# GpSimd's subtraction of weight parts in 128-column instructions, in a two-layer attention and retention trunk

## The chip, the cores and the metric

The kernel runs on one core of a Trainium2 chip. The metric is the device time of one execution in microseconds (us); the median of several runs is compared.

## The reference

Two layers of a decoder trunk over 528 rows (16 learned meta rows ahead of 512 real ones) of width 1024, all in float32. Cut to what matters:

```
h = concatenate([meta, x])                       # (528, 1024)
for each of 2 layers:
    proj = rmsnorm(h) @ w_in                     # 1024 -> 3592 columns
    fq, fk, fv, flog, rq, rk, rv, rg = split(proj)
    fox = softmax(fq fk^T / 8 + c[t] - c[s], causal) fv     # 8 heads of 64; c = cumsum(log_sigmoid(flog + b))
    ret = groupnorm((rotate(rq) rotate(rk)^T * decay) rv)   # 4 heads of 128
    h = h + concatenate([fox, silu(rg) * ret]) @ w_out
    hn = rmsnorm(h)
    h = h + (silu(hn @ w_gate) * (hn @ w_up)) @ w_down      # 1024 -> 2816 -> 1024
return rmsnorm(h)[16:]
```

## The kernel before, in words

Activations lie transposed in SBUF: eight tiles `h0` to `h7` of 128 features by 528 rows. A product is made exact enough by splitting each operand into a high part, rounded to TensorE's fast float32 form, and a low part, the rest. Three products are summed in PSUM: high weights by high activations (`whi`, `xh`), high by low (`whi`, `xl`) and low by high (`wlo`, `xh`).

Weights come in jobs. A job is a block of 128 output columns: 8 slices of 128 by 128, 1024 columns in SBUF. `dense_steps` makes a job and the steps of its 8 slices (`chunk`), `convert` fetches and splits it. For a job:

- SP issues the load of 512 KB into one of three `raw` buffers (`fetch`, L153). It waits until the buffer's former job is split.
- ScalarE rounds the first four slices (128x512) into `whi`, and later the other four (L186).
- The low part is `raw` less `whi`, again for four slices at a time (L187). GpSimd makes it for the jobs with `pool` set, which are nearly all projections of the attention half (`w_in`, part of `w_out`), 63 jobs in all. VectorE makes it for the others. `whi` and `wlo` have two buffers each.
- TensorE takes a slice at a time: `whi` by `xh`, `whi` by `xl`, `wlo` by `xh`, each in one or two parts of the rows (L210).

The split of a job is asked for while TensorE works on the job before it, at its second and its fifth slice (`ahead=(1, 4)`), so TensorE's first use lies some microseconds behind.

The order of TensorE's instructions is a list written out by hand, in which the steps of attention (`fox_steps`) and retention (`ret_steps`) are merged at chosen places among the slices of the projections. The other engines' orders come from a scheduler by priorities. Every engine runs its instructions in order and waits for the others by semaphores.

Names that the text speaks of: `R` is the rows' scale from the norm (L290, L293 on VectorE compute it, and the per-head `r` in the same way); `z` is the forget gate's logarithm, summed over the rows by L393 and written to DRAM as `cdr` (L395), from where it comes back spread over all partitions as `bc` (L487). `scores` adds `bc` to the scores and takes the row minimum `nmax` (L504, L509 joins two halves), and ScalarE takes the exponential (L517). `kl` is the low part of the attention keys (L443), `pd` holds values (L449), `vv` their transposes (L474), `ptl` the low part of the transposed probabilities (L138 in `split`). L613 is the rotation's last sum, L751 and L753 weigh the retention's output by its gate, L760 scales it, L778 adds to `h`.

The feed-forward halves split their weights on ScalarE and VectorE (L863, L864) and have no GpSimd work.

Of the kernel before, what the change touches and what calls it, by code (L numbers as in the profile page):

```python
# [10 lines left out]
F32 = mybir.dt.float32  # L11
# [28 lines left out]
def hybrid_kernel(ctx, tc, x_t, w_in, w_fl, w_out, w_gate, w_up, w_down, vecs, b_fg, rope, decay, mask, ident, out_t):  # L40
# [104 lines left out]
    def fetch(j):  # L145
        job = jobs[j]
        if "load" in job:
            job["load"]()
        elif "raw" not in job:
            n = job["src"].shape[1]  # L150
            job["raw"] = wp.tile([128, NK, 128], F32, name="raw", tag="raw", bufs=3)
            if j > 1:
                nc.sync.dma_start(job["raw"], job["src"]) if n == NK else \  # L153
                    nc.sync.dma_start(job["raw"][:, 0:n], job["src"])

    def wring(tag):
        pool = phase["ffn"] if tag[0] == "f" else wp
        return pool.tile([128, NK, 128], F32R, name=tag, tag=tag, bufs=2)

    def convert(j, upto=NK, pinned=False):  # L160

        if j >= len(jobs):
            return
        job = jobs[j]
        fetch(j)
        if "make" in job:
            if "w" not in job:
                n = job["n"]
                hi, lo = (wring(job["ring"] + p) for p in ("whi", "wlo"))
                job["w"] = [(NK, hi, lo)]  # L170
                job["make"](hi[:, 0:n], lo[:, 0:n])
            return
        n = job["src"].shape[1]
        if "w" not in job:
            job["w"] = job["own"]() if job["own"] else \
                [(NK, *[wp.tile([128, NK, 128], F32R, name=i, tag=i) for i in ("whi", "wlo")])]
            job["split"] = 0
        sub = nc.gpsimd.tensor_sub if job["pool"] else nc.vector.tensor_sub
        while job["split"] < min(n, upto):
            c0 = job["split"]  # L180
            c1 = min(n, c0 + (2 if j < 2 and c0 < 4 else 4))
            size, hi, lo = job["w"][c0 // job["w"][0][0]]
            o = c0 % size
            hi, lo = hi[:, o:o + c1 - c0], lo[:, o:o + c1 - c0]
            with tc.high_priority() if j == 5 else ExitStack():
                pin(nc.scalar.copy(hi, job["raw"][:, c0:c1]), pinned)  # L186
            pin(sub(lo, job["raw"][:, c0:c1], hi.bitcast(F32)), pinned)  # L187
            job["split"] = c1

    def dense_steps(src, parts, pool=False, banks=False, ahead=(1, 4), own=None, wait=None):  # L190
# [6 lines left out]
        def chunk(k0, k, n, xs, cols, ps, done):  # L197
            def go():
                convert(j)
                if k == 0:  # L200
                    t = [psum_a() for _ in cols] if banks else psum()
                    ps.append(t)
                    ps.append(t if banks else [t[:, b] for b in range(2)])
                size = jobs[j]["w"][0][0]
                _, hi, lo = jobs[j]["w"][(k0 + k) // size]
                wk = (k0 + k) % size
                xh, xl = xs(k)
                for i, (w, x) in enumerate(((hi, xh), (hi, xl), (lo, xh))):
                    for b, (c0, c1) in enumerate(cols):
                        nc.tensor.matmul(ps[1][b][:, 0:c1 - c0], w[:, wk, :], x[:, c0:c1],  # L210
                                         start=(k == 0 and i == 0), stop=(k == n - 1 and i == 2))
                if k == n - 1:
                    done(ps[0]) if wait is None else wait.append(lambda: done(ps[0]))
                for half, at_step in enumerate(ahead):
                    if k0 + k == at_step:
                        convert(j + 1, 4 * half + 4)
            return go
# [82 lines left out]
    def pin(f, pinned=True):  # L300
        if pinned:
            tc.keep_in_program_order(f)
# [485 lines left out]
    def ffn(l, st, real, last):  # L788
# [68 lines left out]
        def need(j):  # L857
            for i in range(j, min(j + 3, len(jobs))):
                if i <= j or "make" in jobs[i]:
                    convert(i)  # L860
# [542 lines left out]
```

## Time and profile before

| what | value |
|---|---|
| time, median of 3 runs | 1278.69 us (1278.58 to 1278.84) |
| the profiled execution: time | 1278.89 us |
| the profiled execution: span of the records | 1277.1 us |
| TensorE busy | 1258.0 us |
| VectorE busy | 1019.4 us |
| ScalarE busy | 687.7 us |
| GpSimd busy | 181.0 us, 172.3 of it in the 126 subtracts of L187 |
| mean granted TensorE clock | 0.996 |

In a row of instructions stand the line, the engine, the operation, what it writes and reads, and its size. Behind it come the total, the mean in ns, and the idle time just before, with what ended it. In a row of the timeline stand the start, the duration and the count, and in brackets the idle time before and what ended it. PE is TensorE, PEld its weight loads, DVE VectorE, ACT ScalarE, POOL GpSimd, SPq the queue of SP, which issues the DMAs. Rows of one instruction that follow each other are merged in the timeline (x2), the start being the first one's.

### The profile page before, as it was taken

What the parts mean: (1) busy time and instruction counts of PE and PEld (TensorE: products, weight loads), DVE (VectorE), ACT (ScalarE), POOL (GpSimd) and SP (SyncE); (2) the same over time, 40 slices, a digit from 0 to 9 for tenths busy, and PEclk for the clock granted to TensorE, in tenths of its full rate; (3) what the DMA queues carried; (4) which work ended last, traced back from release to release, by engine and by line L of the source; (5) the groups of instructions that cost most, each with busy time, mean ns of one, the idle gap of its engine ahead of it and who ended that gap; (6) DMA issues with size and microseconds to landing.
All of it is one profiled execution on the core that took longest, in us unless ns stands there. A gap on an engine that the chain in (4) does not pass through costs nothing.

```text
span 1277.1 us, 23190 instructions
## 1 busy us (share of the span) xinstructions
PE 1258.0 (99%) x9265; PEld 1197.8 (94%) x9265; DVE 1019.4 (80%) x1849; ACT 687.7 (54%) x1250; POOL 181.0 (14%) x150
## 2 busy tenths in 40 slices
PE   9999999999999999999999999999999999999997
PEld 8899999999999999999999989999789999999996
DVE  7888866879988888887687878568899878888867
ACT  7566655576544444444455665456764444444445
POOL 2233333210000000000014334332000000000001
PEclk9999999999999999999999999999999999999998
DMA  6222222223323333332323122222223333333321
GB/s 233 76 67 84 75 84 84 66 73 115 107 97 100 100 100 100 100 100 83 100 76 112 65 100 84 77 91 66 100 83 130 102 100 100 100 100 100 103 79 67
DMA packets 45677, 120.55 MB, mean 94 GB/s; under 512 B 5360, under 2 KB 12272, under 8 KB 45568
## 3 DMA queue, kind: packets, MB, share of 16 engines
q1 hardware_dynamic: 45136, 118.77, 28.4%
q8 instruction: 73, 1.20, 0.4%
q10 hardware_dynamic: 432, 0.29, 0.1%
q14 instruction: 36, 0.29, 0.1%
HBM read 116.91 MB, written 2.13 MB: 93 GB/s over the span
## 4 chain that ended last, share of the span: by engine, by line
PE 84%; DVE 10%; ACT 4%; DMA 1%; issue 1%; DVEq 0%; POOL 0%; ACTq 0%
PE psd L210 24%; PE psa L875 18%; PE psd L1010 14%; PE psd L875 13%; PE psa L1010 4%; PE psa L210 3%; PE psa L409 2%; PE psa L497 1%; PE psa L567 1%; PE psa L724 1%; PE psa L694 1%; DVE qs L429 1%; DMA bc<-cdr 1%; DVE pr L504 1%; DVE rsl L138 0%
## 5 line engine op out<-in xcount | busy, mean ns | idle before, releaser
L187 POOL TENSOR_TENSOR wlo<-raw,whi 128x512 fp32r<-128x512 f32 x126 | 172.3, 1381 | 380.2 <-ACT whi L186 380.2
L210 PE MATMUL psd<-xh,whi 128*128 128x264 f32 (+1 forms) x792 | 195.8, 315 | 0.0
L210 PE MATMUL psd<-xl,whi 128*128 128x264 f32 (+1 forms) x792 | 186.5, 303 | 0.6 <-DVE xl L313 0.6
L210 PE MATMUL psd<-xh,wlo 128*128 128x264 f32 (+1 forms) x792 | 186.9, 303 | 0.0
L210 PEld LDWEIGHTS psd<-xh,whi 128*128 128x128 f32 x792 | 128.7, 190 | 4.7 <-ACT whi L186 0.4
L210 PEld LDWEIGHTS psd<-xh,wlo 128*128 128x128 f32 x792 | 127.2, 188 | 6.2 <-DVE wlo L187 0.4
L210 PEld LDWEIGHTS psd<-xl,whi 128*128 128x128 f32 x792 | 128.0, 189 | 5.2 <-DVE xl L313 1.2
L186 ACT CAST whi<-raw 128x512 fp32r<-128x512 f32 (+1 forms) x168 | 98.3, 613 | 39.2 <-PE psd L210 19.9
L863 ACT CAST whi<-raw 128x1024 fp32r<-128x1024 f32 (+2 forms) x62 | 54.9, 885 | 51.3 <-PE psd L875 39.9
L863 ACT CAST fwhi<-raw 128x1024 fp32r<-128x1024 f32 (+2 forms) x62 | 55.6, 897 | 48.1 <-PE psd L875 40.5
L864 DVE TENSOR_TENSOR wlo<-raw,whi 128x1024 fp32r<-128x1024 f32 (+2 forms) x62 | 62.9, 1014 | 13.7 <-ACT whi L863 13.6
L864 DVE TENSOR_TENSOR fwlo<-raw,fwhi 128x1024 fp32r<-128x1024 f32 (+2 forms) x62 | 64.0, 1032 | 10.8 <-ACT fwhi L863 10.5
L875 PE MATMUL psa<-th,whi 128*128 128x264 f32 (+1 forms) x232 | 65.4, 282 | 0.0
L875 PE MATMUL psa<-th,wlo 128*128 128x264 f32 (+1 forms) x232 | 65.4, 282 | 0.0
L875 PE MATMUL psa<-tl,whi 128*128 128x264 f32 (+1 forms) x232 | 65.3, 282 | 0.0
L875 PE MATMUL psa<-th,fwhi 128*128 128x264 f32 (+1 forms) x224 | 63.4, 283 | 0.0
L875 PE MATMUL psa<-tl,fwhi 128*128 128x264 f32 (+1 forms) x224 | 63.3, 283 | 0.0
L875 PE MATMUL psa<-th,fwlo 128*128 128x264 f32 (+1 forms) x224 | 63.3, 282 | 0.0
L517 ACT ACTIVATE pr<-pr,nmax 128x144 f32<-128x144 f32 (+1 forms) x64 | 36.9, 576 | 42.8 <-DVE nmax L504 30.5
L941 ACT COPY e<-psa 128x264 f32<-128x264 f32 (+1 forms) x114 | 42.9, 376 | 27.9 <-PE psa L875 23.6
L863 ACT CAST fwhi<-S 128x1024 fp32r<-128x1024 f32 x20 | 21.0, 1049 | 68.6 <-PE psa L875 66.5
L1010 PE MATMUL psd<-ah,fwlo 128*128 128x264 f32 (+1 forms) x200 | 56.6, 330 | 0.0
(355 smaller groups left out, 4008.6 us busy)
## 6 DMA issues: line engine op xcount, KB each, us to landing
raw<-w_in SPq DMA_DIRECT2D x54, 512.0 KB, 3.5
raw<-w_gate SPq DMA_DIRECT2D x44, 512.0 KB, 4.0
fraw<-w_up SPq DMA_DIRECT2D x38, 512.0 KB, 3.4
raw<-w_down SPq DMA_DIRECT2D x64, 256.0 KB, 2.7
raw<-w_out SPq DMA_DIRECT2D x16, 512.0 KB, 3.5
raw<-w_down SPq DMA_DIRECT2D x32, 192.0 KB, 2.5
bc<-cdr SPq DMA_DIRECT2D x16, 264.0 KB, 3.3
raw<-w_up SPq DMA_DIRECT2D x6, 512.0 KB, 3.5
```

Source lines behind the costliest of these rows:

```text
L186: pin(nc.scalar.copy(hi, job["raw"][:, c0:c1]), pinned)
L187: pin(sub(lo, job["raw"][:, c0:c1], hi.bitcast(F32)), pinned)
L210: nc.tensor.matmul(ps[1][b][:, 0:c1 - c0], w[:, wk, :], x[:, c0:c1], start=(k == 0 and i == 0), stop=(k == n - 1 and i == 2))
L409: nc.tensor.transpose(ps[:, 128 * j:128 * j + 128], src[:, o:o + 128], idt)
L429: nc.vector.tensor_sub(sv(t, real, b0, b1), sv(tq, real, a0, a1), sv(t, real, a0, a1).bitcast(F32))
L497: nc.tensor.matmul(sc[0:nq, 0:c1 - c0], st["q"][s][:, q0:q0 + nq], kk[:, c0:c1], start=(i == 0), stop=(i == 1))
L517: nc.scalar.activation(pr, pr, AF.Exp, bias=nmax[0:nq], scale=-1.0, accum_out=rsum)
L863: nc.scalar.copy(hi, src)
L864: nc.vector.tensor_sub(lo, src, hi.bitcast(F32))
L875: nc.tensor.matmul(bank()[:, 0:b.shape[-1]], a[:, o + k, :], b, start=(fresh and k == 0 and i == 0), stop=(k == n - 1 and i == 2), skip_gr ...
L941: nc.scalar.copy(self.t["e"][:, i], self.t["x"][:, 0:w])
L1010: nc.tensor.matmul(v[:, 0:c1 - c0], a[:, s * n + k, :], b[:, c0:c1], start=(k == 0 and i == 0), stop=(k == n - 1 and i == 2))
```

## The change

Where GpSimd subtracts, the four slices of a half job are taken one by one: four instructions of 128x128 in the place of one of 128x512. VectorE's subtracts stay as they are.

```
-            pin(sub(lo, job["raw"][:, c0:c1], hi.bitcast(F32)), pinned)
+            step = 1 if job["pool"] else c1 - c0
+            for c in range(0, c1 - c0, step):
+                pin(sub(lo[:, c:c + step], job["raw"][:, c0 + c:c0 + c + step], hi[:, c:c + step].bitcast(F32)), pinned)
```

On GpSimd, the first job's two halves before (lines of the changed kernel are two higher from here on):

```order
L187 TENSOR_TENSOR wlo<-raw,whi 128x512 [waits DVE_49,DMAHW1_49,PE_49,Activation_49]
L187 TENSOR_TENSOR wlo<-raw,whi 128x512 [waits Activation_49]
L187 TENSOR_TENSOR wlo<-raw,whi 128x512 [waits DVE_49,DMAHW7_49,PE_49,Activation_49]
L187 TENSOR_TENSOR wlo<-raw,whi 128x512 [waits Activation_49]
L187 TENSOR_TENSOR wlo<-raw,whi 128x512 [waits DMAHW2_49,PE_49,Activation_49]
```

and now:

```order
L189 TENSOR_TENSOR wlo<-raw,whi 128x128 [waits DVE_49,DMAHW1_49,PE_49,Activation_49]
L189 TENSOR_TENSOR wlo<-raw,whi 128x128 x3
L189 TENSOR_TENSOR wlo<-raw,whi 128x128 [waits Activation_49]
L189 TENSOR_TENSOR wlo<-raw,whi 128x128 x3
L189 TENSOR_TENSOR wlo<-raw,whi 128x128 [waits DVE_49,DMAHW7_49,PE_49,Activation_49]
L189 TENSOR_TENSOR wlo<-raw,whi 128x128 x3
```

The first piece of four has the waits of the whole, the other three have none.

On TensorE, a job of the first layer, before; `xh_168`, `xh_176` and so on are the activations' slices:

```order
L210 MATMUL psd<-xh_180,wlo 128x264 x2
L210 MATMUL psd<-xh_188,whi 128x264 x2
L210 MATMUL psd<-xl_189,whi 128x264 x2
L210 MATMUL psd<-xh_188,wlo 128x264 [waits Pool_49]
L210 MATMUL psd<-xh_188,wlo 128x264
```

and now:

```order
L212 MATMUL psd<-xh_180,wlo 128x264 [waits Pool_49]
L212 MATMUL psd<-xh_180,wlo 128x264
L212 MATMUL psd<-xh_188,whi 128x264 x2
L212 MATMUL psd<-xl_189,whi 128x264 x2
L212 MATMUL psd<-xh_188,wlo 128x264 [waits Pool_49]
L212 MATMUL psd<-xh_188,wlo 128x264
```

The matmuls stand in the same order; each slice of `wlo` now has a wait for GpSimd, where the first and the fifth had one.

On SP's queue, the second layer's loads around `cdr`, before:

```order
L153 DMA raw<-w_in 128x1024 [waits DMAHW3_49,Pool_49]
L153 DMA raw<-w_in 128x1024 [waits DMAHW4_49,Pool_49]
L395 DMA cdr_8437<-z_8429 8x528 [waits DVE_49]
L487 DMA bc<-cdr_8437 128x528 [waits DMAHW3_49]
L487 DMA bc<-cdr_8437 128x528 [waits DMAHW5_49]
```

and now:

```order
L153 DMA raw<-w_in 128x1024 [waits DMAHW3_49,Activation_49,Pool_49]
L153 DMA raw<-w_in 128x1024 [waits DMAHW4_49,Activation_49,Pool_49]
L397 DMA cdr_8623<-z_8615 8x528 [waits DVE_49]
L489 DMA bc<-cdr_8623 128x528 [waits DMAHW3_49]
L489 DMA bc<-cdr_8623 128x528 [waits DMAHW5_49]
```

The order is the same, with `cdr` and `bc` behind a load that waits for GpSimd; a wait for ScalarE's reading of the same buffer is added. VectorE's and ScalarE's instructions keep their order too.

## The prediction

> **What bounds the kernel now.** I read the page's first part, then the table by stretches, then the rows of GpSimd and of the weight matmuls.
>
> ```profile
> span 1277.1 us, 23190 instructions
> PE 1258.0 (99%) x9265; PEld 1197.8 (94%) x9265; DVE 1019.4 (80%) x1849; ACT 687.7 (54%) x1250; POOL 181.0 (14%) x150
> ...
> L187 POOL TENSOR_TENSOR wlo<-raw,whi 128x512 fp32r<-128x512 f32 x126 | 172.3, 1381 | 380.2 <-ACT whi L186 380.2
> ...
> L210 PE MATMUL psd<-xl,whi 128*128 128x264 f32 (+1 forms) x792 | 186.5, 303 | 0.6 <-DVE xl L313 0.6
> L210 PE MATMUL psd<-xh,wlo 128*128 128x264 f32 (+1 forms) x792 | 186.9, 303 | 0.0
> ```
>
> TensorE fills the span, so the change counts only where TensorE now stands idle. GpSimd is busy for 14% of the span and its subtracts stand in two stretches only, the attention halves of the two layers:
>
> ```profile
> 0.00:305.00 305.00, 296.53 (x2356) 291.15 (x2357) 239.88 (x558) 188.07 (x414) 84.72 (x70) 0.99 0.30 97
> ...
> 650.00:910.00 260.00, 259.04 (x1679) 234.09 (x1679) 191.51 (x413) 155.44 (x328) 88.97 (x64) 1.00 0.24 80
> ```
>
> The columns are time, then TensorE, weight loads, VectorE, ScalarE and GpSimd. Do TensorE's stalls there come from GpSimd? Directly only one: among all that weight loads wait for, this is GpSimd's only row.
>
> ```profile
> PEld psa L210 <- POOL wlo L187: 0.5, 1, 0.5
> ```
>
> Indirectly there are more. A VectorE instruction that reads two operands from SBUF does not run while GpSimd is inside a subtract. In the timeline:
>
> ```profile
> 103.95 1.28 POOL L187 TENSOR_TENSOR wlo<-raw,whi 128x512 fp32r<-128x512 f32 x1
> 103.98 1.27 DVE L509 TENSOR_TENSOR nmax<-nmax 128x1 f32<-128x1 f32 x1
> 105.28 0.74 ACT L517 ACTIVATE pr<-pr,nmax 128x528 f32<-128x528 f32 x1 [1.51 <-DVE nmax L509]
> 108.08 0.41 PE L409 MATMUL psa<-idt,pr 128*128 128x128 f32 x2 [1.14 <-DVE psa L503]
> ...
> 124.56 0.16 DVE L509 TENSOR_TENSOR nmax<-nmax 128x1 f32<-128x1 f32 x1
> ```
>
> One column takes VectorE 0.16 us when GpSimd rests, and 1.27 us when it comes 0.03 us behind a subtract: it ends with it. ScalarE's exponential waits for it, and TensorE stands for 1.14 us at the end of that chain. So what decides is how long one GpSimd instruction holds VectorE off.
>
> **The change part by part.** *The pieces.* 126 instructions of 512 columns become 504 of 128. The trace has no two-operand GpSimd instruction of 128 columns. I bound it by a pair with a VectorE instruction between:
>
> ```profile
> 24.27 3.02 POOL L187 TENSOR_TENSOR wlo<-raw,whi 128x512 fp32r<-128x512 f32 x2 [0.43 <-ACT whi L186]
> 24.77 1.36 DVE L290 TENSOR_TENSOR nwt<-R 128x528 f32<-128x528 f32 x1 [1.45 <-ACT R L289]
> 26.97 0.88 DVE L293 SCALAR_TENSOR_TENSOR R<-nwt,R 128x528 f32<-128x528 f32 x1
> ...
> L187 POOL TENSOR_TENSOR wlo<-raw,whi x126: 1268/1296/2902, 21.3 to 901.9; 128x512 fp32r<-128x512 f32 x126
> L358 POOL MEMSET mxh<- 128x512 f32 x2 | 1.0, 524 | 0.0
> L109 POOL MEMSET rs<- 128x16 f32 x4 | 0.2, 104 | 0.0
> L613 DVE TENSOR_TENSOR tq<-tq,xsw x16: 680/1080/1689, 49.6 to 872.0; 128x528 f32<-128x528 f32 x12, 128x512 f32<-128x512 f32 x4
> ```
>
> The pair ends at 27.29, the VectorE instruction at 26.13, so VectorE got in between the two although the second was already queued. The second ended 1.16 us behind it, 0.13 us under the undisturbed 1.296: that much is start-up that can be waited through. With 0.13 fixed, a piece is 0.13 + 1.16/4 = 0.42 us, four are 1.7 (or 1.55 where start-ups overlap). The lower bound is a fixed cost of 0.10, the smallest GpSimd instruction (104 ns): 0.40 a piece, the group about the old 1.3 where start-ups overlap. The upper bound takes the slope of the memset, (524 - 104)/496 = 0.85 ns a column, and leaves 0.86 us fixed: 0.97 a piece, 3.9 a group. I take 0.42, as its row is of the same instruction. So GpSimd's busy time goes to about 205 us, and an instruction of VectorE with two SBUF operands is held for at most 0.3 us (0.42 less start-up) where it lost up to 1.1 (680 ns at best for L613, 1689 at worst).
>
> [...]
>
> *TensorE's waits.* Some 370 more weight loads carry a wait for their own piece. Satisfied waits cost nothing: 303 ns for the `wlo` matmuls, which hold the present waits, and 303 for `xl`, which hold almost none. As each matmul waits for its own 128 columns, the first need is met by a 0.42 us piece rather than a 1.3 us one. What hides the longer group is the consumption, in the next rows 0.73 us from one slice of `wlo` to the next, against 0.42 for a piece; without that cover the price would be 0.4 us a group.
>
> ```profile
> 120.82 0.31 PEld L210 LDWEIGHTS psd<-xh,wlo 128*128 128x128 f32 x2
> 121.55 0.31 PEld L210 LDWEIGHTS psd<-xh,wlo 128*128 128x128 f32 x2
> ```
>
> *ScalarE and SP.* 26 ScalarE and 13 SP sequencer waits are added, on work long done and off the path. The raw buffers are freed up to 0.4 us later; their loads are early, as ScalarE waits for them only twice:
>
> ```profile
> ACT whi L186 <- DMA raw<-w_in: 1.2, 2, 0.7
> ```
>
> *The stalls that shrink.* Each term is what VectorE loses now, less what it will lose, capped by TensorE's stall. The order on VectorE, ScalarE and TensorE stays.
>
> ```profile
> 35.19 0.18 PE L497 MATMUL psa<-kl,qs 128*16 128x16 f32 x1 [0.76 <-DVE kl L443]
> ...
> 56.60 1.28 POOL L187 TENSOR_TENSOR wlo<-raw,whi 128x512 fp32r<-128x512 f32 x1 [1.85 <-ACT whi L186]
> 57.36 1.08 DVE L613 TENSOR_TENSOR tq<-tq,xsw 128x528 f32<-128x528 f32 x1
> 59.10 0.51 PE L567 MATMUL psa<-ptl,vv 128*128 128x512 f32 x1 [1.75 <-DVE ptl L138]
> ...
> 92.52 1.69 DVE L293 SCALAR_TENSOR_TENSOR r<-nwt,r 128x528 f32<-128x528 f32 x1
> 95.41 0.89 PE L409 MATMUL psa<-idt,pd 128*128 128x128 f32 x5 [0.88 <-DVE pd L449]
> ...
> 146.06 1.68 DVE L753 TENSOR_TENSOR d<-d,sg 128x528 f32<-128x528 f32 x1
> 150.55 1.77 DVE L293 SCALAR_TENSOR_TENSOR r<-nwt,r 128x528 f32<-128x528 f32 x1
> 157.60 0.51 PE L210 MATMUL psd<-mxh,whi 128*128 128x264 f32 x2 [0.90 <-DVE h L778]
> ...
> 901.88 1.62 POOL L187 TENSOR_TENSOR wlo<-raw,whi 128x512 fp32r<-128x512 f32 x1 [3.12 <-ACT whi L186]
> ```
>
> 1. At 35.19 TensorE waits for keys at the end of a VectorE chain from `R`. L290 and L293 lost 0.68 and 0.20; in pieces about 0.2 each at most. Gain 0.5 of the 0.76.
> 2. At 59.10: L613 lost 0.40, and came 0.76 us into the subtract, by then at a boundary. Gain 0.35.
> 3. At 95.41: L293 lost 1.0; a piece costs it 0.2, and the L760 behind it 0.2. Gain 0.6.
> 4. At 108.08: L509 lost 1.1, now at most 0.42. Gain 0.8.
> 5. At 157.60: L753 and L293 lost 2.1; less 0.5, more than the stall. Gain 0.9, all of it.
> 6. At 903.55, the direct wait: the first piece is there 0.7 us sooner. Gain 0.3 of the 0.5.
> 7. The second layer's small stalls behind `sql` and the like: 0.3, an estimate.
>
> Together 3.75 us. What is late next in each case is TensorE's own stream, or the next VectorE link.
>
> *One place turns worse.* In the second layer four subtracts meet the cumulative sum, and SP's queue stands behind them:
>
> ```profile
> 661.21 12.72 SPq L153 DMA_DIRECT2D raw<-w_in  x2
> 669.42 7.14 POOL L187 TENSOR_TENSOR wlo<-raw,whi 128x512 fp32r<-128x512 f32 x4 [8.23 <-ACT whi L186]
> 669.59 2.23 DVE L393 TENSOR_TENSOR_SCAN z<-z 8x528 f32<-8x528 f32 x1
> 671.76 2.40 DVE L443 TENSOR_TENSOR kl<-tq,kh 64x528 fp32r<-64x528 f32 x2
> 673.99 0.32 SPq L395 DMA_DIRECT2D cdr<-z  x1
> 680.55 0.31 DVE L504 CUSTOM_DVE_ANT_0 pr<-psa,bc 128x144 f32<-128x144 f32 x1 [1.99 <-DMA bc<-cdr]
> 684.69 0.30 PE L409 MATMUL psa<-idt,pd 128*128 128x128 f32 x1 [0.64 <-DVE vv L474]
> ```
>
> `z` is summed by 671.82, yet its DMA leaves at 673.99: ahead of it on SP stands a load of `raw`, which waits until GpSimd has ended its second subtract (two whole ones in a row take 2.6 us, these two about 4.2 with what VectorE holds them up; the load's issue ends at 673.93). In pieces this second group ends later: eight pieces are 0.8 us longer than two whole ones, and VectorE's second L443, held off until now, cuts in for about 0.6; the piece that was under way gives 0.3 back. So +1.1 for the DMA, less 0.4 that the chain ahead gains as in term 1: +0.7 on the wait for `bc` and on TensorE's 0.64. Bounds: -0.3 (pieces at 0.40 with overlap, sum earlier) and +1.3; far more at 0.97 a piece.
>
> **Sum.** -3.75 + 0.7 = -3.05. The profiled execution took 1278.89 (span 1277.1 and 1.8 around it), 0.2 over the median of 1278.69. From the median: 1275.6 us.
>
> **The rivals.**
> - *The gains are taken back* (0.36): a freed VectorE instruction finds ScalarE or a later piece in its way, terms 1 to 5 yield half (1.6 for 3.15), and the SP place costs its full 1.3. Then -1.6 - 0.6 + 1.3 = -0.9, 1277.8. For it: TensorE's idle time is small, and stalls of one chain overlap. Against: terms 3 to 5 rest on losses of 1.0 and more each.
> - *Queued pieces keep the port* (0.06): if GpSimd's next piece is taken ahead of a waiting VectorE instruction, this waits for all four, 1.7 rather than 1.3. Eight held instructions on the chains named lose 0.4 more, 1.3 + 0.3 on SP's place less term 6: 1278.7 + 3.2 + 0.7 = 1282.6, slower. It decides at the boundary between two pieces. The pair at 24.27 speaks against it: there VectorE got in.
> - *Dear pieces* (0.04): 0.97 each. VectorE's holds fall to 0.84 at most, so some 1 us is gained, and the second group at 669 ends 5 us later; 1278.7 - 1 + 4 = 1281.7.
> - The change does what it says: 504 pieces stand on GpSimd's queue. That nothing at all moves is within the first rival.
>
> **How the numbers follow.** The forecast has 0.54. About 0.2% (2.56 us, the boundary 1276.1) is what a measurement of this kernel can tell. The forecast reaches from 1273.2 (terms 1 and 3 to 5 at their stalls' full 3.7, term 2 at its 0.4, term 6 at 0.5, term 7 doubled, the SP place at -0.3) to 1276.4 (SP at +1.3, 0.2 more elsewhere), so a little of it is "same". Faster 0.53, same 0.37 (the first rival and that end of the forecast), slower 0.10. The range for 8 in 10 leaves out the two slow rivals and what of the first lies above it: 1273.2 to 1278.6.
>
> **What would show it.** GpSimd's pieces near 0.42 us, and VectorE's busy time down by 15 to 25 us; L613's and L293's longest near 1.0 instead of 1.7. TensorE's stalls at 95, 108 and 157 gone or halved; GpSimd no longer among those that weight loads wait for; `cdr` in the second layer leaving later behind the start of its group, and the stall at 684 longer. The prediction is wrong if VectorE's longest holds stay near 1.7 us, if pieces are over 0.6 us, or if other releasers stand at the same stalls.

## The result, and the profile after

| | before | after |
|---|---|---|
| median | 1278.63 us | 1271.76 us |
| ratio (95% interval) | | 0.9954 (0.9942 to 0.9967) |
| profiled execution | 1278.89 us, span 1277.1 | 1271.49 us, span 1269.7 |

The change makes the kernel 6.9 us faster by the medians. The forecast was a gain of 3.05, and its range ended at 5.5: the direction was right, the size was not.

The profile's page after, first part and GpSimd's group, then three answers by line (duration in ns as minimum/median/maximum). L189 is the subtract, L615 the former L613, L295 the former L293.

```profile
span 1269.7 us, 23607 instructions
PE 1253.9 (99%) x9265; PEld 1196.3 (94%) x9265; DVE 998.5 (79%) x1849; ACT 688.3 (54%) x1250; POOL 270.3 (21%) x528
L189 POOL TENSOR_TENSOR wlo<-raw,whi 128x128 fp32r<-128x128 f32 x504 | 261.6, 556 | 285.1 <-ACT whi L186 285.1
```
```profile
L189 POOL TENSOR_TENSOR wlo<-raw,whi x504: 445/464/2073, 21.3 to 896.7; 128x128 fp32r<-128x128 f32 x168
L615 DVE TENSOR_TENSOR tq<-tq,xsw x16: 680/708/1025, 48.9 to 865.1; 128x528 f32<-128x528 f32 x12, 128x512 f32<-128x512 f32 x4
L295 DVE SCALAR_TENSOR_TENSOR r<-nwt,r x8: 675/702/857, 87.4 to 892.7; 128x528 f32<-128x528 f32 x4, 128x512 f32<-128x512 f32 x4
```

A piece takes 464 ns in the median. VectorE does the same 1849 instructions in 20.9 us less, and its longest holds are gone: the sum L613 went from 1080 ns in the median and 1689 at worst to 708 and 1025. GpSimd's own busy time rose by 89 us; TensorE pays for it at the two negative places of the next table, and with a smaller win at 35.19.

Where did TensorE win? Both kernels start the same 9265 matmuls in the same order, so the step from one start to the next can be subtracted matmul by matmul. The differences gather at few places (time in the trace before; plus is won, us; places under 0.2 are left out where they have no forecast, so the rows don't add up to the whole). The last two columns are two experiments from below.

| place | forecast | after | 256 columns | no subtract |
|---|---|---|---|---|
| start, 5.8 to 8.0 | - | 0.32 | 0.27 | 0.30 |
| 35.19 (term 1) | 0.5 | 0.21 | 0.26 | 0.86 |
| 59.10 (term 2) | 0.35 | 1.03 | 0.41 | 1.14 |
| 61.21 to 64.45 | - | 1.53 | 1.53 | 1.52 |
| 84.98 | - | 0.39 | 0.39 | 0.39 |
| 95.41 (term 3) | 0.6 | 1.22 | 0.74 | 1.22 |
| 108.08 (term 4) | 0.8 | 1.33 | 0.96 | 1.33 |
| 157.60 (term 5) | 0.9 | 1.17 | 0.00 | 1.17 |
| 246.44 | - | -0.32 | -0.15 | 0.27 |
| 684.69 (SP's place) | -0.7 | -1.07 | -0.29 | 0.80 |
| 709, 722, 851, 874 (term 7) | 0.3 | 1.04 | 0.67 | 1.24 |
| 903.55 (term 6) | 0.3 | 0.33 | 0.33 | 0.33 |
| whole trace | 3.05 | 7.40 | 5.29 | 8.96 |

One row was in no part of the prediction: 61.21 to 64.45. There is no stall in it. Twelve matmuls in a row start 220 ns apart where they start 121 apart in the trace after. The stretches of the two traces (time, TensorE, weight loads, VectorE, ScalarE, GpSimd, then TensorE's granted clock, the busy share of the DMA engines and their GB/s), of before and of after:

```profile
57.54:60.95 3.41, 1.85 (x13) 1.80 (x14) 2.36 (x5) 1.92 (x6) 0.34 (x1) 1.00 0.43 154
60.95:64.37 3.42, 3.42 (x18) 3.42 (x17) 1.86 (x6) 0.49 (x2) 0.00 (x0) 0.50 0.01 4
```
```profile
56.98:60.39 3.41, 2.72 (x20) 2.69 (x21) 2.10 (x7) 1.56 (x6) 0.77 (x2) 1.00 0.38 142
60.39:63.81 3.42, 3.42 (x31) 3.42 (x30) 3.12 (x12) 2.12 (x5) 1.18 (x3) 1.00 0.33 79
```

Before, TensorE's granted clock is 0.50 for 3.41 us, right behind the stretch in which the stall of 59.1 leaves it busy for only 1.85 us. After, the stall is a microsecond shorter and the clock stays at 1.00.

### The profile page after: what moved, and what is told of

Read it like the earlier page. It is cut to its first block, busy times and chain, and to the rows that moved or that the text cites. A ratio compares the mean times of both kernels' runs of the same rounds, so it can differ in the third digit from the quotient of the medians.

```text
span 1269.7 us, 23607 instructions
## 1 busy us (share of the span) xinstructions
PE 1253.9 (99%) x9265; PEld 1196.3 (94%) x9265; DVE 998.5 (79%) x1849; ACT 688.3 (54%) x1250; POOL 270.3 (21%) x528
## 4 chain that ended last, share of the span: by engine, by line
PE 95%; DVE 2%; DMA 1%; ACT 1%; issue 0%; DVEq 0%; ACTq 0%; SPq 0%
PE psd L212 31%; PE psa L877 18%; PE psd L1012 14%; PE psd L877 13%; PE psa L212 5%; PE psa L1012 4%; PE psa L411 2%; PE psa L569 2%; PE psa L499 2%; PE psa L726 1%; PE psa L696 1%; PE psa L375 1%; DMA bc<-cdr 1%; PE psa L285 0%; DMA cdr<-z 0%; DMA raw<-w_in 0%
## 5 line engine op out<-in xcount | busy, mean ns | idle before, releaser
L189 POOL TENSOR_TENSOR wlo<-raw,whi 128x128 fp32r<-128x128 f32 x504 | 261.6, 556 | 285.1 <-ACT whi L186 285.1
L1112 POOL TENSOR_TENSOR th<-th,e 128x544 f32<-128x544 f32 x2 | 2.9, 1458 | 359.6 <-ACT sq L1105 359.6
```

The costliest lines, as they stand in the source:

```text
L189: pin(sub(lo[:, c:c + step], job["raw"][:, c0 + c:c0 + c + step], hi[:, c:c + step].bitcast(F32)), pinned)
```

## The experiments

A hold is the time that a VectorE instruction loses while it waits for GpSimd's subtract to end. Theory: the holds add up along VectorE's queue, also where the held instruction is far ahead of the stall; shorter subtracts shorten all of them. Rivals: only the last held instruction of a chain counts (so the prediction sized its terms); or the finer waits of the weight loads bring the gain.

### Which layer

```diff
# against the changed kernel; e_layer1 (jobs below 100 are the first layer's)
-            step = 1 if job["pool"] else c1 - c0
+            step = 1 if job["pool"] and j < 100 else c1 - c0
# e_layer2
+            step = 1 if job["pool"] and j > 100 else c1 - c0
```

> Pieces of 128 columns in the first layer's attention half alone; the second layer's GpSimd subtracts stay at 512. Theory (the holds of VectorE behind GpSimd's subtracts add up along VectorE's queue, and the first layer has nearly all of them that TensorE feels): 6.5 to 7.5 us under before, that is all of the whole change's gain or a little more, since the place in the second layer at which SP's queue waits for GpSimd stays as it was (stall at 684.7 near 0.8 us instead of 1.9). Rival (only the last held instruction of each chain counts, the sizing of the prediction): 2.8 to 3.5 us under before. Rival (the second layer's 66 changed groups give their share): 3 to 4 us, half of the whole.

> Pieces of 128 columns in the second layer alone. By the trace of the full change the second layer wins 1.4 us at small stalls (709, 722, 851, 874, 904) and loses 1.1 at 684.7, where cdr leaves SP's queue late; the stall at 59.1 and the half clock behind it stay. Theory: 0 to 0.8 us under before, two groups of times as before. Rival (each changed group is worth the same): 3 to 3.7 us under before, half of the whole.

Measured: the first layer alone 1272.61 us, ratio 0.9953 (0.9940 to 0.9965), which can't be told from the whole change; that is 6.3 us under the before of the same runs, a little less than the 6.5 to 7.5 expected. The second alone 1277.81, ratio 0.9996 (0.9987 to 1.0005), no difference that shows. In the first layer's trace every row of the table from 59.10 to 157.60 is the whole change's to 0.01 us and the second layer's are within 0.08 of none. In the second layer's trace the small stalls give 1.4 us and the place at 684.69 takes 1.7 back; why it is 0.6 more there than in the whole change stays open. Both rivals (2.8 to 4 us for the first layer) fall, also when the 1.5 of the half clock is taken off the 6.3.

### No subtract on GpSimd

```diff
# e_nohold, against the kernel before
-            pin(sub(lo, job["raw"][:, c0:c1], hi.bitcast(F32)), pinned)
+            if job["pool"]:
+                for _ in range(3):
+                    pin(nc.gpsimd.memset(lo.bitcast(F32), 0.0), pinned)
+            else:
+                pin(sub(lo, job["raw"][:, c0:c1], hi.bitcast(F32)), pinned)
```

> Left out: the low parts of the weights that GpSimd makes. In place of each subtract of 512 columns GpSimd fills the same 512 columns of wlo with zeros, three times over, near 0.52 us each and 1.6 us in all, so that it reads nothing from SBUF, has the same columns ready in one group (no finer waits) and is as long busy as before. Theory (holds): VectorE's longest L293 and L613 fall to near their free time of 0.7 to 0.9 us and TensorE's time falls by at least as much as with the pieces, 6 to 9 us under before; were writes to hold VectorE as well, then by 0.5 us each, and 5 to 7. Rival (what brings the gain is that each weight load waits for its own 128 columns and the first come earlier): 0 to 1 us, since the groups stay whole.

Measured: 1270.04 us, ratio 0.9933 (0.9920 to 0.9945), 8.9 us under before. Page and lines:

```profile
PE 1254.4 (99%) x9265; PEld 1196.3 (94%) x9265; DVE 985.6 (78%) x1849; ACT 688.3 (54%) x1250; POOL 188.6 (15%) x402
L189 POOL MEMSET wlo<- 128x512 f32 x378 | 179.9, 532 | 356.4 <-PE psd L214 329.5
```
```profile
L617 DVE TENSOR_TENSOR tq<-tq,xsw x16: 680/699/710, 49.4 to 863.5; 128x528 f32<-128x528 f32 x12, 128x512 f32<-128x512 f32 x4
```

GpSimd is busy as long as before (188.6 for 181.0), in whole groups without finer waits, and all of the gain is there: the rival of the finer waits falls. L613 (here L617) now lies within 680 to 710 ns. That row alone does not show that a fill leaves VectorE alone, since of the 16 only one has a fill under way, for 0.08 us. The low part of the keys, `kl`, shows it: seven of its 16 instructions have a fill under way for more than 0.1 us and take 0.67 to 0.70 us (one in the first two rows below), where beside subtracts the same instruction took up to 1.69 (last row). But L538, a multiply of a 16x16 tile, which takes 0.21 to 0.22 us with no fill beside it, took 1.58 beside a row of them and ended with the last:

```profile
83.52 1.45 POOL L189 MEMSET wlo<- 128x512 f32 x3
84.33 0.69 DVE L447 TENSOR_TENSOR kl<-tq,kh 64x528 fp32r<-64x528 f32 x1
215.07 2.84 POOL L189 MEMSET wlo<- 128x512 f32 x6 [3.76 <-PE psd L214]
216.35 1.58 DVE L538 TENSOR_SCALAR pm<-pm,rsum 16x16 f32<-16x16 f32 x1
```
```profile
L443 DVE TENSOR_TENSOR kl<-tq,kh x16: 670/706/1692, 34.5 to 828.0; 64x528 fp32r<-64x528 f32 x16
```

So the fills did not hold `kl`, which subtracts held for up to 1.0 us, and they held L538, of another kind, for 1.36. The fill also no longer waits for ScalarE or for `raw`, so that it runs at other times and SP's place is eased too; the first layer's rows in the table are free of that place.

### Which hold reaches the stall

```diff
# against the changed kernel; e_near and near5: of the groups ahead of 59.1, the last alone
-            step = 1 if job["pool"] else c1 - c0
+            step = 1 if job["pool"] and (j, c0) == (7, 4) else c1 - c0
# e_far: the three ahead of it alone
+            step = 1 if job["pool"] and (j, c0) in ((6, 0), (6, 4), (7, 0)) else c1 - c0
```

> The kernel before, with pieces of 128 columns in one group alone: the one at 56.6 us, into which L613 at 57.36 falls, the last VectorE instruction of that chain that GpSimd holds. TensorE's excess over its usual spacing at the stall of 59.1 us is 1.99 us before and 0.96 with all groups in pieces. Theory (holds add up along VectorE's queue): it falls by 0.35 to 0.4 us, what this L613 loses, and no more. Rival (only the last hold counts, and the full change won more there for another reason, such as earlier weights): the same 0.35 to 0.4, and the next run, without this group, 0. Rival (one later link is enough): 0.9 to 1.0.

> The kernel before, with pieces of 128 columns in the three groups ahead of that one alone (45.9, 49.2 and 53.5 us); the group at 56.6, next to the stall, stays whole. Theory: L138 at 46.1 and L613 at 49.6, held by these groups, pass what they win on along VectorE's queue, 1.0 us by 49.6, of which 0.6 to 0.7 arrives at the stall of 59.1 (1.99 before; 1.3 to 1.4 here). Rival (slack on the way, only the last held instruction counts, as the prediction's second term has it): the stall stays within 0.1 of 1.99.

In brackets is TensorE's wait at the stall (1.75 before). The first two rows are of the last group alone, the next two of the three farther ones, the last of the whole change:

```profile
56.87 0.70 DVE L615 TENSOR_TENSOR tq<-tq,xsw 128x528 f32<-128x528 f32 x1
58.23 0.51 PE L569 MATMUL psa<-ptl,vv 128*128 128x512 f32 x1 [1.39 <-DVE ptl L138]
```
```profile
57.10 1.09 DVE L615 TENSOR_TENSOR tq<-tq,xsw 128x528 f32<-128x528 f32 x1
58.85 0.50 PE L569 MATMUL psa<-ptl,vv 128*128 128x512 f32 x1 [1.10 <-DVE ptl L138]
```
```profile
57.67 0.50 PE L569 MATMUL psa<-ptl,vv 128*128 128x512 f32 x1 [0.71 <-DVE ptl L138]
```

The last hold is worth 0.36, the three farther ones 0.65, all of them 1.04. They add, and the farther ones are the larger part, although L613 next to the stall still takes 1.09 us in the second kernel. The rival by which only the last hold counts falls.

The way of the farther win is not VectorE's queue alone, as the theory had it. Between the farther holds and the stall VectorE stands idle for 1.28 us and waits for ScalarE, before and with the farther groups in pieces alike:

```profile
51.04 0.64 ACT L137 CAST rqh<-tq 128x528 fp32r<-128x528 f32 x1 [1.27 <-DVE tq L613]
55.42 0.71 DVE L610 TENSOR_TENSOR xsw<-xsw,sr 128x528 f32<-128x528 f32 x1 [1.28 <-ACT xsw L609]
```
```profile
50.69 0.64 ACT L137 CAST rqh<-tq 128x528 fp32r<-128x528 f32 x1 [0.86 <-DVE tq L615]
55.17 0.71 DVE L612 TENSOR_TENSOR xsw<-xsw,sr 128x528 f32<-128x528 f32 x1 [1.29 <-ACT xsw L611]
```

VectorE hands the win to ScalarE, whose wait for L613 shrinks from 1.27 to 0.86 us, and ScalarE hands it back.

### The half clock

```diff
# again1, again2: the kernel before, unchanged
```

> The kernel before, unchanged, profiled once more. In its first profile TensorE's granted clock is 0.50 from 60.95 to 64.37 us, right behind the stall of 1.99 us at 59.1, and TensorE is 1.53 us behind its usual spacing there; no run of a kernel with a shorter stall at this place shows that. Theory (the grant is judged in a fixed grid of 3.41 us, whose place in the program differs from run to run, and the stall decides it only where it falls into one of these windows with enough of its length): a time near 1278.9 comes with a half-clock stretch of 3.41 us there, a time near 1277.4 without one; all other stalls are within 0.1 us of the first profile. Rival (the stretch has another cause, such as which memory is being loaded): it is there in every execution, or times do not go with it.

> As the run ahead of it, a third execution of the kernel before: near 1278.9 us with a half-clock stretch of 3.41 us behind the stall at 59.1, or near 1277.4 us without one.

> The kernel before with the one group at 56.6 us in pieces, timed in several runs. Theory: the hold gives 0.36 us; besides, with 1.63 us of excess instead of 1.99 TensorE is busy for more of any window of 3.41 us at this place, so that the half clock behind it comes in fewer runs or none: all runs within 0.5 us of each other, 1.0 to 2.0 us under the median of before. Rival (the half clock does not depend on the length of this stall): two groups of times as before, the median 0.3 to 0.5 us under it.

Stretches of the first repeat of the kernel before, and of the kernel with pieces in the second layer alone, whose first layer is the same:

```profile
55.01:58.42 3.41, 2.24 (x18) 1.93 (x17) 3.09 (x7) 2.32 (x7) 1.28 (x1) 1.00 0.00 0
58.42:61.84 3.42, 2.83 (x21) 2.79 (x22) 2.12 (x6) 1.28 (x3) 0.00 (x0) 1.00 0.45 153
```
```profile
56.45:59.86 3.41, 1.67 (x11) 1.31 (x11) 3.39 (x8) 1.84 (x6) 1.27 (x1) 1.00 0.20 24
59.86:63.28 3.42, 3.42 (x18) 3.41 (x17) 0.88 (x3) 0.58 (x1) 0.00 (x0) 0.50 0.32 129
```

The repeats took 1277.12 and 1278.08 us and have no half clock; in both the only first-layer gain over the first profile is 1.52 at 61.21 to 64.45, with the stall itself the same (the second lost 0.5 at 39.75 and 0.5 at the start). So the same program, with the same loads at this place, has the half clock in one execution and not in two others. The half clock of before lasts 3.41 us (60.95 to 64.37), and the clock changes stand a whole multiple of 3.413 us apart in each trace (54.61 us, 16 times that, from the first full clock to the half clock, in both traces that have it here). The grid of this step begins at another moment in each execution: the half clock starts at 60.95 us in the first profile of before and at 59.86 in that of the second-layer kernel. Where the stall fell into one stretch of the grid (1.85 and 1.67 us busy of 3.41) half clock followed; where the grid cut it in two (2.24 and 2.83, in the second repeat 2.55 and 2.52) it did not. The busy time of a stretch alone does not decide it in these traces: the second-layer kernel has a stretch with 1.62 us busy, 684.50 to 687.92, and no half clock behind it, while at the end of the changed kernel 2.04 us busy, 1258.47 to 1261.88, has one. What else decides it was not shown.

The timed runs of the last group alone (near5) fit neither expectation: median 1277.39, ratio 0.9990 (0.9981 to 0.9999), more than the hold's 0.36 us, but spread over 1276.3 to 1278.4. None of the three traces of a kernel with that stall shortened (two of this one, one of e_far) has a half clock; how often it comes in runs without a trace stays open. Of the 21 runs of before timed beside these, nine have a mean clock of 0.998 and average 1277.8 us, twelve have 0.996 or 0.997 and average 1279.0.

### The size of the piece, and SP's queue

```diff
# e_256
-            step = 1 if job["pool"] else c1 - c0
+            step = 2 if job["pool"] else c1 - c0
# e_64: two instructions of 64 columns for each 128
```

> Pieces of 256 columns in both layers, two to a group. A piece should take 0.71 to 0.75 us (between the 0.45 of 128 columns and the 1.29 of 512). Theory (holds): the time lost by held VectorE instructions lies between 41 us (512) and 23 us (128), near 30, and the time is 3.5 to 5.5 us under before. Rival (only the last held instruction counts): 1.5 to 2 us. Rival (finer waits): the first 128 columns come with the second at 0.73 us, still ahead of what the first layer needs, so nearly the full gain of 7.

> Pieces of 64 columns in both layers, eight to a group. By the line through 0.45 us (128) and 1.29 us (512) a piece takes 0.31 us and the group 2.5 us instead of 1.8 to 1.9. Theory (holds): each hold is at most 0.3 us, but GpSimd is busy for some 90 us longer and more VectorE instructions meet it; 6 to 8 us under before, with the place in the second layer (SP's load waiting for GpSimd) worse than with 128, its stall 2.3 us or more. Rival (the shorter the better, without limit): 9 us under before. Rival (GpSimd's own time is what counts in the end): under 5.

```profile
L189 POOL TENSOR_TENSOR wlo<-raw,whi x252: 715/740/2356, 21.5 to 897.8; 128x256 fp32r<-128x256 f32 x126
```
```profile
L190 POOL TENSOR_TENSOR wlo<-raw,whi x1008: 312/323/2140, 21.4 to 907.0; 128x64 fp32r<-128x64 f32 x168
```

256 columns: 1273.60 us, ratio 0.9966 (0.9953 to 0.9978), as the theory has it, between before and the change, as is VectorE's busy time (1008.2 us); at 157.60 it wins nothing, since five VectorE instructions ahead of it (L755, L445, L292, L295, L762) still take 1.13 to 1.24 us each for some 0.7. 64 columns: 1282.01 us, ratio 1.0027 (1.0016 to 1.0038), slower than before, which no theory had (6 to 8 us faster was expected). VectorE is busy for less than with 128, 992.9 us, so the holds are not it. The timeline of 64 columns at the first layer's cumulative sum:

```profile
20.77 16.52 SPq L153 DMA_DIRECT2D raw<-w_in  x3
21.41 19.98 POOL L190 TENSOR_TENSOR wlo<-raw,whi 128x64 fp32r<-128x64 f32 x48 [19.48 <-ACT whi L186]
32.52 1.24 DVE L398 TENSOR_TENSOR_SCAN z<-z 8x528 f32<-8x528 f32 x1
37.38 0.30 SPq L400 DMA_DIRECT2D cdr<-z  x1
44.74 0.59 PE L502 MATMUL psa<-kh,qs 128*128 128x272 f32 x1 [6.37 <-DVE nmax L509]
```

`z` is summed by 33.76. SP's queue stands behind a load of `raw` until 37.3, because the buffer is freed by GpSimd's subtracts, which now run without a pause from 21.4 to 41.4. In the trace before, `cdr` left at 34.57. TensorE stands for 6.4 us, and has half clock for 6.8 in and behind it, from 40.80 to 47.62. It is the place that the prediction named in the second layer, come up in the first. Two kernels take the DMA of the sum off that queue, one with 128 columns (second layer only), one with 64:

```diff
# e_cdr, and e64_cdr in both layers (there also the first layer's first loads of bc)
-        nc.sync.dma_start(st["cdr"], z2)
+        (nc.scalar if l else nc.sync).dma_start(st["cdr"], z2)
```

> The changed kernel, with the DMA of the second layer's cumulative sum on ScalarE's queue instead of SP's, so that it no longer stands behind a load of raw that waits for GpSimd. Theory (this place costs the change 1 to 2 us): cdr leaves near 664.2 instead of 668.3, bc near 668.3 instead of 671.4, TensorE's excess near 679 falls from 1.88 to under 0.5, and the time is 8 to 9.5 us under before, 1 to 2 under the changed kernel. Rival (the loads of bc wait behind the same queue item anyway): bc not before 671, excess 1.5 or more, time as the changed kernel. Rival (ScalarE's queue pays for the DMA and its wait): the excess goes, and as much turns up elsewhere.

> Pieces of 64 columns, with the DMA of the cumulative sum on ScalarE's queue in both layers, and the first two loads of bc of the first layer too. With 64 columns alone the time was 3.1 us over before: TensorE's excess is 6.5 us at 44.7 us, where cdr left SP's queue at 37.4 instead of 34.1, and 2.8 us around 685. Theory (64 columns lose at these two queue places alone): excess at 44.7 under 2.5 and around 685 under 0.8; time 3 to 6 us under before. Rival (so many instructions of GpSimd cost VectorE or the weight loads more everywhere): the two stalls shrink, and the time stays within 1.5 us of before.

The second layer's place, of the whole change and then with the DMA on ScalarE's queue:

```profile
655.55 12.65 SPq L153 DMA_DIRECT2D raw<-w_in  x2
662.35 8.84 POOL L189 TENSOR_TENSOR wlo<-raw,whi 128x128 fp32r<-128x128 f32 x16 [6.83 <-ACT whi L186]
662.53 1.40 DVE L395 TENSOR_TENSOR_SCAN z<-z 8x528 f32<-8x528 f32 x1
668.25 0.32 SPq L397 DMA_DIRECT2D cdr<-z  x1
671.42 0.81 SPq L489 DMA_DIRECT2D bc<-cdr  x2
678.76 0.30 PE L411 MATMUL psa<-idt,pd 128*128 128x128 f32 x1 [1.71 <-DVE vv L476]
```
```profile
663.02 1.40 DVE L395 TENSOR_TENSOR_SCAN z<-z 8x528 f32<-8x528 f32 x1
664.45 0.53 ACTq L397 DMA_DIRECT2D cdr<-z  x1
668.80 0.90 SPq L489 DMA_DIRECT2D bc<-cdr  x2
```

With the change alone `cdr` waits for 4.3 us from the end of the sum (663.93) and TensorE for 1.71; moved, `cdr` leaves 0.03 us behind the sum, `bc` 3.1 us sooner after it, and the stall is gone (0.80 won at 684.69 over before, where the change lost 1.07). The time is 1270.18 us, ratio 0.9935 (0.9922 to 0.9947), 1.6 under the change and the fastest of all with the whole computation. With 64 columns the same move gives 1270.73, ratio 0.9941 (0.9928 to 0.9955), 8.2 us under before for 3 to 6 expected: 11 us from one queue's order. Between the two traces of 64 columns TensorE's steps differ at the two places alone, by 6.8 us around 40 (with the half clock there) and by 3.7 around 685. So the rival of dear GpSimd instructions falls, and nothing turned up elsewhere.

## Why the prediction was wrong in size

**The mechanism was right.** VectorE's busy time fell by 20.9 us (15 to 25 forecast), L613's and L293's longest fell to 1025 and 857 ns (near 1.0), the stalls at 95, 108 and 157 are gone, GpSimd is no longer among those that weight loads wait for. The rival of queued pieces falls: a held instruction would have waited for four of them, and L613's longest is 1025 ns. (Read as they stand, that rival's terms sum to 1283.2 and not to its 1282.6.)

**The piece.** 0.42 us was taken, 0.464 was measured, 0.04 above it and far under the upper bound of 0.97. With the three sizes more, 323, 464, 740 and 1296 ns lie on a line: 0.18 us and 2.17 ns a column. GpSimd's busy time came out at 270 us and not 205, in part by the longer piece and in larger part because pieces wait for VectorE in their turn: 104 of the 504 take more than 0.5 us (2073 ns at worst), each beside an instruction of VectorE.

**Terms 2 to 5 are the step that failed**, in both halves of the rule that opens them: what the held instructions lose, and the cap by TensorE's stall. The four gave 4.75 us for 2.65 forecast.

The first half took the last held instructions alone. Term 2 counted L613 at 57.36 (0.35) and won 1.03; the three groups farther ahead gave 0.65 of it. Term 3 counted L293 at 92.52 and the L760 behind it; before them VectorE loses 0.98 at L750 and 0.48 at L751, and in the trace after both are free (L752 and L753). VectorE runs there without a pause, so these holds can reach the stall, but no run takes them one by one. Before, and then after:

```profile
85.58 1.68 DVE L750 SCALAR_TENSOR_TENSOR gr<-ge,gr 128x528 f32<-128x528 f32 x1
87.80 1.18 DVE L751 TENSOR_TENSOR sg<-sg,gr 128x528 f32<-128x528 f32 x1
```

```profile
81.27 0.71 DVE L752 SCALAR_TENSOR_TENSOR gr<-ge,gr 128x528 f32<-128x528 f32 x1
82.51 0.70 DVE L753 TENSOR_TENSOR sg<-sg,gr 128x528 f32<-128x528 f32 x1
87.36 0.86 DVE L295 SCALAR_TENSOR_TENSOR r<-nwt,r 128x528 f32<-128x528 f32 x1
98.81 0.18 DVE L511 TENSOR_TENSOR nmax<-nmax 128x1 f32<-128x1 f32 x1
```

Term 4 put L509's hold at up to 0.42; it takes 0.18 (last row), near the 0.14 to 0.18 of before when GpSimd rests.

The second half took the idle time in the brackets for the whole stall. It is not: ahead of the matmuls at 95.41, 108.08 and 157.60 the step from one start to the next fell from 1.16, 1.42 and 1.18 us to 0.12, that is by 0.16 more than the brackets' 0.88, 1.14 and 0.90, and the matmuls right behind gain a little more. So term 5, which had counted on all of its 0.90, still gave 1.17. Of the 2.1 us that the four terms missed, 0.8 lie above the caps and 1.3 in holds that were not counted or, in term 4, put too high for the time after.

Term 7, an estimate without rows of its own, gave 1.04 for 0.3, and 84.98 gave 0.39 unforeseen.

**The half clock was not in the sum.** 1.53 us of the 7.40 between the two profiled executions is the granted clock behind the stall of 59.1. Set against the repeat of before without it, the trace after is 5.64 us shorter, still 2.6 over the forecast's gain.

**Term 1 was too large**, 0.21 for 0.5, and 246.44 turned 0.32 worse: a chain that meets GpSimd's longer series of pieces is held a little at several links. Ahead of 35.19, L290 wins 0.61, but the two L429 behind it now take 1.74 us for 1.44, and L391 0.57 for 0.48. Ahead of 246.44, L613 wins 0.47, and three instructions behind it lose 0.25 to 0.28 each. Without subtracts term 1 gives 0.86.

**The place on SP's queue** was named rightly, with its cause; it cost 1.07 for 0.7, within the bound of 1.3. The rival that the gains are taken back (0.36) did not come: besides this place only 246.44 took any back.

## What to carry to other kernels

Where one engine holds another off, don't price only the held instruction next to the stall: holds farther ahead can arrive there too, also over a third engine, and at the one stall taken apart here they add (0.36 and 0.65 of 1.04 us). Price a stall by the step from start to start, before against a place that flows, and not by the idle time in the profile's bracket, which was 0.16 us too small at three stalls. Shorten the holding instruction until the hold is under the slack, but look at what its own longer queue frees late: a DMA that stands behind a buffer's release can cost more than all holds together (11 us with 64 columns, where 8.2 are won without that wait), and moving it to another queue is one line or two. And look at the granted clock behind each long stall in a fine window, since the page's slices of 32 us hide a stretch of 3.4.

## What the hardware showed unexpectedly

TensorE's granted clock was 0.50 for 3.41 us behind a stall of 2 us in one of three traced executions of the same program; there the stall lay in one stretch of a grid of 3.41 us, in the other two the grid cut it. It is worth 1.5 us. A GpSimd fill, which reads nothing, did not hold the two-operand `kl` on VectorE (0.67 to 0.70 us beside fills), a GpSimd subtract did (up to 1.69 us for the same); but a 16x16 multiply took 1.58 us beside fills instead of 0.22. Two of the six runs of the changed kernel took 1273.7 and 1274.3 us, the others 1271.5 to 1271.8; with `cdr` moved all five lie within 0.3 us. The mean granted clock of these two is 0.997, as in two of the four others, and no trace of such a run was taken, so the cause stays open.
